# Layer 0's second and third modulation banks: 64 TensorE products per layer replaced by VectorE sums in the loaded tiles

## The chip, the core and the metric

The kernel runs on one core of a Trainium2 chip. A core has a matrix engine (TensorE, PE in the profile; its weight loads are the rows PEld), a vector engine (VectorE, DVE), a scalar engine (ScalarE, ACT), GpSimd (POOL) and a queue engine that issues most transfers (SyncE, SP). Each engine works through its own list of instructions in order and waits on semaphores. The metric is the device time of one execution in microseconds.

## The reference

Two decoder layers on 512 tokens of width 1024, in fp32. Each layer first makes six modulation rows of width 1024 from one conditioning vector `c`, and it is this product that the change touches:

```python
cond = jax.nn.silu(c)
mod = cond @ w_ada[l] + b_ada[l]              # w_ada[l]: 1024 x 6144
sh1, sc1, g1, sh2, sc2, g2 = jnp.split(mod, 6)
h = x * (1 + sc1) + sh1
y = hybrid_mixer(h, ...)                      # w_in, three token mixers, w_out
x = layer_norm(alpha * x + g1 * y)
h = x * (1 + sc2) + sh2
x = layer_norm(alpha * x + g2 * conv_ffn(h))
```

The mixer has a gated MLP, a retention (four chunks) and a sparse attention with eight heads, and ends in the product with w_out. In layer 0, `sh1` and `sc1` are needed at the very start, `sh2`, `sc2` (bank 1) and `g1`, `g2` (bank 2) only behind the mixer.

## The kernel before

Each weight tile of 128x1024 fp32 (512 KB) is loaded into one of three buffers `wraw` by SP (`Weights.load`, L102), and most are then split into a high part (ScalarE, L125) and a low part (VectorE or GpSimd, L127), so that three fast products give nearly fp32 accuracy. The modulation weights are used as they are loaded (jobs marked "raw"): row 8p+k of `w_ada` lies on partition p of tile k, so tile (k, h) holds one eighth of the contraction for the h-th 1024 columns of a bank.

`ada_bank` (L315) makes banks 1 and 2 of layer 0, 16 tiles each: for each tile, two fp32 products (L324) with `ce[:, k]` (silu of c) spread over 32 columns as the stationary side, 512 columns each, added up in PSUM over k. The four 512-wide pieces go to four 32-row strips of one PSUM bank. `ada_finish` (L357) adds the bias, and for bank 1 transposes.

These steps are fillers: `attention()` yields pieces of the attention (32 units: 4 head pairs, 2 branches, 4 row blocks; scores L944 to L946, row maximum L952, exponential L955, scaling L959, transposes L990, product with the values L998), between which `filler()` puts one piece of the retention (projections L535 to L537, chunks L881 to L920) and, at the places of `ADA_AT`, one modulation step. Attention looks two units ahead (`LOOK`). The unit whose row block is the first stands for both branches (L970 to L982). The written order is then rearranged by the framework's own scheduler, which puts instructions on each engine by its estimate of when they are ready; so the order on an engine is not that of the text.

`ada_dve` (L328) makes the banks of layer 1 another way, inside layer 0's feed-forward stage: GpSimd issues the loads, VectorE multiplies and adds each tile into an accumulator (L340, L342), and one product per strip with a column of ones sums over the partitions (L346).

The order of jobs for SP's queue: the eight tiles of the retention's projections (`rq` to `rg`) with the 32 modulation tiles between and behind them, then eight of w_out.

Of the kernel before, what the change touches and what calls it, by code (L numbers as in the profile page):

```python
# [14 lines left out]
OP = mybir.AluOpType  # L15
AX = mybir.AxisListType

P = 128
# [3 lines left out]
KD = D // P  # L22
# [126 lines left out]
def tile_trunk(ctx, tc, I, tab, out, layers=L):  # L149
    nc = tc.nc  # L150
    V, A, G, T = nc.vector, nc.scalar, nc.gpsimd, nc.tensor
# [6 lines left out]
    def ps():  # L158
        return psum.tile([P, 512], F32, tag="ps", name="ps")

    def t2(dt=F32):
        return pool.tile([P, 512], dt, tag="t2", name="t2", bufs=4)
# [44 lines left out]
    ADA_RUNS = {0: (0, D), 1: (3 * D, 4 * D), 2: (2 * D, 5 * D)}  # L207
# [9 lines left out]
    def ada_jobs(l, bank):  # L217
        wa = I["w_ada"][l].rearrange("(p k) n -> p k n", k=KD)
        return [(("ada", l, bank, k, h), "raw", [(lambda t: t[:, :D], wa[:, k, c0:c0 + D])])
                for k in range(KD) for h, c0 in enumerate(ADA_RUNS[bank])] + [None, None]  # L220

    def job_tm(key, l, parts):
        for h in range(2):
# [8 lines left out]
    for l in range(layers):  # L232
# [13 lines left out]
        for b, c0 in enumerate((C_KSL, C_KWN)):  # L246
            job_cols(("k", l, b), l, [(c0, P)])
        aj = [j for bank in (1, 2) for j in ada_jobs(l, bank)] if l == 0 else []
        for n in range(32):
            if n % 8 in (0, 2):  # L250
                nm, c0 = (("rq", C_QB), ("rk", C_KB), ("rv", C_VB), ("rg", C_GB))[n // 8]
                h = n % 8 // 2
# [14 lines left out]
    ws = Weights(nc, wpool, jobs)  # L267
# [5 lines left out]
    ce = const.tile([P, KD], F32, name="ce")  # L273
# [29 lines left out]
    ones = const.tile([P, 32], F32, name="ones")  # L303
# [10 lines left out]

    def ada_bank(l, bank):  # L315

        pm = ps()
        bt = ada_bias(l, bank)
        for k in range(KD):
            for h in range(2):  # L320
                raw = ws.next(("ada", l, bank, k, h))
                for a2 in range(2):
                    a = 2 * h + a2
                    T.matmul(pm[32 * a:32 * a + 32, :], ce[:, k:k + 1].to_broadcast([P, 32]), raw[:, a2 * 512:(a2 + 1) * 512],  # L324
                             start=(k == 0), stop=(k == KD - 1), tile_position=(0, 32 * a))
                yield
        yield from ada_finish(l, bank, pm, bt)

# [22 lines left out]
    def ada_bias(l, bank):  # L351
        bt = pool.tile([P, 512], F32, tag="adab", name="adab", bufs=1)
        for a in range(4):
            c0 = ADA_RUNS[bank][a // 2] + 512 * (a % 2)
            nc.gpsimd.dma_start(bt[32 * a:32 * a + 32, :], I["b_ada"][l][None, c0:c0 + 512].to_broadcast([32, 512]))
        return bt

    def ada_finish(l, bank, pm, bt):
        ms = pool.tile([P, 512], F32, tag="modg", name="modg", bufs=1) if bank == 2 else bt
        V.tensor_tensor(ms, pm, bt, op=OP.add)  # L360
        res = ms
        yield
        if bank != 2:

            pc = ps()
            for j in range(4):
                T.transpose(pc[:, j * P:(j + 1) * P], ms[:, j * P:(j + 1) * P], ident)
            res = pool.tile([P, 2, KD], F32, tag="modc", name="modc", bufs=3)
            V.tensor_copy(res.rearrange("p s (a j) -> p (s a) j", j=4),
                          pc.rearrange("p (j s x) -> p s j x", j=4, s=4)[:, :, :, 0])  # L370
            V.tensor_scalar(res[:, 1, :], res[:, 1, :], 1.0, None, op0=OP.add)
        ada_out[l, bank] = res
        yield
# [135 lines left out]
    for l in range(layers):  # L509
# [77 lines left out]
        else:  # L587
# [20 lines left out]
            def start_acc(k):  # L608

                r = raws.pop(k)  # L610
                acc = pt()[:, :256].rearrange("p (s n) -> p s n", s=2)
                for k2 in range(KD):
                    if k2 == 0:
                        V.tensor_scalar(acc, r[:, 0], ce[:, 0:1], None, op0=OP.mult)
                    else:
                        V.scalar_tensor_tensor(acc, r[:, k2], ce[:, k2:k2 + 1], acc, op0=OP.mult, op1=OP.add)
                return acc
# [36 lines left out]
            for k in range(KD):  # L654
# [7 lines left out]
                if k + 1 < KD:  # L662
                    ws.split(k + 1)
                    acc = start_acc(k + 1)
# [562 lines left out]
        for ct in range(NFF):  # L1227
# [8 lines left out]
            for b in range(2):  # L1236
                pa = pas[b]
                a = t2()
# [136 lines left out]
```

## Time and profile before

| | us |
|---|---|
| median of 3 runs (lowest, highest) | 1427.34 (1426.94, 1430.43) |
| the profiled execution, its own time | 1429.17 |
| its span, from the first to the last instruction | 1427.2 |
| PE busy in the span | 1368.5 |
| DVE busy | 889.6 |
| ACT busy | 549.4 |
| POOL busy | 213.8 |

A busy share is an average over stages with different limits; stages are told apart by the views of a stretch of time (counted in us from the span's start). The stage of the change runs from about 117 us, where the attention of layer 0 begins, to 324 us, where the residual add behind w_out begins.

### The profile page before, as it was taken

Reading aid. Unit: us, or ns where it says so; the run is one execution under the profiler, and the core shown is the slowest. Engines: PE = TensorE matmul, PEld = TensorE weight load, DVE = VectorE, ACT = ScalarE, POOL = GpSimd, SP = SyncE. Lnnn points to the kernel's source line nnn. Section 1 sums busy time; section 2 is a strip of 40 time slices with the busy share of each in tenths; the row PEclk is TensorE's granted clock in tenths of the full one; section 3 lists DMA queues with packets and bytes.
Section 4 is the critical chain, followed back from the end, with each engine's and each line's share of the span. In section 5 each row is a group of like instructions: output and inputs, shape, how many; then the busy total and the mean of one; then the engine's idle time right before and its main releaser. Section 6 shows DMA issues by size and latency. Waiting matters only on the chain.

```text
span 1427.2 us, 19802 instructions
## 1 busy us (share of the span) xinstructions
PE 1368.5 (96%) x7794; PEld 1126.6 (79%) x7794; DVE 889.6 (62%) x1463; ACT 549.4 (38%) x999; POOL 213.8 (15%) x212
## 2 busy tenths in 40 slices
PE   6999999999899999999999989999999999999995
PEld 5898665679887788778879978877898888888884
DVE  6658436757899566843466577486566555764337
ACT  2425333552443343333324245456243334343220
POOL 0311220335211010000030023111510000000005
PEclk9999999999999999999999999999999999999998
DMA  9822454513988354422514131110323334332221
GB/s 280 220 71 89 148 163 155 170 47 91 315 283 265 99 170 124 142 92 89 149 29 118 43 103 45 45 45 30 89 62 94 97 95 127 96 125 90 102 75 59
DMA packets 188012, 168.91 MB, mean 118 GB/s; under 512 B 23526, under 2 KB 167758, under 8 KB 187920
## 3 DMA queue, kind: packets, MB, share of 16 engines
q1 hardware_dynamic: 180368, 141.18, 33.0%
q0 software_dynamic: 7552, 26.48, 5.5%
q8 instruction: 61, 1.00, 0.3%
q14 instruction: 31, 0.25, 0.1%
HBM read 163.44 MB, written 2.10 MB: 116 GB/s over the span
## 4 chain that ended last, share of the span: by engine, by line
PE 83%; DVE 7%; DMA 4%; issue 2%; POOL 1%; ACT 1%; SPq 1%; DVEq 0%; ACTq 0%; POOLq 0%
PE ps L446 19%; PE ps L447 19%; PE ps L445 19%; PE ps L535 4%; PE ps L536 4%; PE ps L537 4%; PE ps L998 3%; PE ps L324 2%; PE ps L990 2%; DMA a<-in_w_ada_dram 1%; PE ps L944 1%; PE ps L506 1%; PE ps L945 1%; DMA wraw<-in_w_up_dram 1%; PE ps L431 1%
## 5 line engine op out<-in xcount | busy, mean ns | idle before, releaser
L125 ACT CAST whi<-wraw 128x1024 fp32r<-128x1024 f32 (+4 forms) x188 | 186.6, 997 | 390.7 <-PE ps L446 208.2
L127 DVE TENSOR_TENSOR wlo<-wraw,whi 128x1024 fp32r<-128x1024 f32 (+3 forms) x162 | 187.4, 1159 | 184.0 <-ACT whi L125 183.6
L447 PE MATMUL ps<-h2h,wlo 128*128 128x512 f32 (+1 forms) x736 | 278.8, 379 | 0.0
L446 PE MATMUL ps<-h2l,whi 128*128 128x512 f32 (+1 forms) x736 | 277.6, 377 | 0.0
L445 PE MATMUL ps<-h2h,whi 128*128 128x512 f32 (+1 forms) x736 | 277.5, 378 | 0.0
L445 PEld LDWEIGHTS ps<-h2h,whi 128*128 128x128 f32 x736 | 138.9, 189 | 28.4 <-ACT whi L125 2.5
L446 PEld LDWEIGHTS ps<-h2l,whi 128*128 128x128 f32 x736 | 139.0, 189 | 27.1
L447 PEld LDWEIGHTS ps<-h2h,wlo 128*128 128x128 f32 x736 | 139.0, 189 | 26.1 <-issue 0.8
L535 PE MATMUL ps<-whi,hh 128*128 128x256 f32 (+1 forms) x448 | 131.7, 294 | 0.0
L536 PE MATMUL ps<-wlo,hh 128*128 128x256 f32 (+1 forms) x448 | 128.1, 286 | 0.0
L537 PE MATMUL ps<-whi,hl 128*128 128x256 f32 (+1 forms) x448 | 127.5, 285 | 0.0
L1141 POOL TENSOR_TENSOR xa<-xa,t 128x256 f32<-128x256 f32 (+1 forms) x30 | 35.8, 1200 | 527.2 <-DVE t L1140 527.2
L446 PE MATMUL ps<-wlo,pt 128*128 128x512 f32 x288 | 113.9, 396 | 0.0
L445 PE MATMUL ps<-whi,pt 128*128 128x512 f32 x288 | 113.9, 396 | 0.0
L447 PE MATMUL ps<-whi,pt 128*128 128x512 f32 x288 | 111.8, 396 | 0.0
L535 PEld LDWEIGHTS ps<-whi,hh 128*128 128x128 f32 x448 | 85.6, 191 | 15.2 <-issue 11.7
L536 PEld LDWEIGHTS ps<-wlo,hh 128*128 128x128 f32 x448 | 85.5, 191 | 3.6 <-issue 3.5
L537 PEld LDWEIGHTS ps<-whi,hl 128*128 128x128 f32 x448 | 85.4, 191 | 0.2 <-issue 0.2
L127 POOL TENSOR_TENSOR wlo<-wraw,whi 128x1024 fp32r<-128x1024 f32 x26 | 62.5, 2406 | 142.7 <-ACT whi L125 142.7
L187 DVE TENSOR_TENSOR pt<-g,pt 128x512 fp32r<-128x512 f32 x32 | 22.1, 691 | 81.5 <-PE ps L446 79.9
L991 ACT COPY pT<-ps 128x128 f32<-128x128 f32 (+3 forms) x128 | 50.2, 438 | 53.3 <-PE ps L990 52.9
L955 ACT ACTIVATE pt<-ps,sm 128x256 f32<-128x256 f32 (+2 forms) x96 | 55.8, 590 | 37.3 <-DVE sm L952 26.1
(272 smaller groups left out, 2682.4 us busy)
## 6 DMA issues: line engine op xcount, KB each, us to landing
wraw<-in_w_up_dram SPq DMA_DIRECT2D x88, 512.0 KB, 3.9
araw<-in_w_ada_dram POOLq DMA_DIRECT2D x48, 512.0 KB, 5.9
wraw<-in_w_down_dram SPq DMA_DIRECT2D x44, 512.0 KB, 3.5
wraw<-in_w_ada_dram SPq DMA_DIRECT2D x32, 512.0 KB, 3.4
wraw<-in_w_in_dram SPq DMA_DIRECT2D x30, 512.0 KB, 3.6
wraw<-in_w_out_dram SPq DMA_DIRECT2D x16, 512.0 KB, 4.1
a<-in_w_ada_dram SPq DMA_DIRECT2D x14, 512.0 KB, 7.2
wraw<-in_w_in_dram SPq DMA_DIRECT2D x8, 384.0 KB
```

The lines of the kernel that those rows point to most:

```text
L125: self.nc.scalar.copy(f(hi), src)
L127: eng.tensor_tensor(f(lo), src, f(hi).bitcast(F32), op=OP.subtract)
L445: T.matmul(o, lh, rh, start=first, stop=False)
L446: T.matmul(o, lh, rl, start=False, stop=False)
L447: T.matmul(o, ll, rh, start=False, stop=last)
L535: T.matmul(o, a, wh[:, k - k0, :], start=(first and k == 0), stop=False)
L536: T.matmul(o, a, wl[:, k - k0, :], start=False, stop=False)
L537: T.matmul(o, b, wh[:, k - k0, :], start=False, stop=(last and k == KD - 1))
L955: A.activation(pp[e][:, :n], o[e], AF.Exp, bias=sm[:, 0, e:e + 1], accum_out=sm[:, 1, e:e + 1])
L991: A.copy(PT[e][:, i:i + 3 * i + 1:3, :], pb[:, :(i + 1) * P].rearrange("p (j q) -> p j q", q=P))
L998: T.matmul(po[64 * e:64 * e + 64, j * P:], VS[:, b, j, 64 * g:64 * g + 64], PT[e][:, 4 * j:4 * j + NT - j, :].rearrange("p a q -> p (a q)" ...
L1141: eng.tensor_tensor(X[t][:, c0:c0 + n], X[t][:, c0:c0 + n], tmp, op=OP.add)
```

## The change

The steps of a bank are put in another order (all eight k of the first half of the columns, then all eight of the second, instead of both halves for each k), and so are their loads. VectorE multiplies the first tile of a half by `ce[:, 0]` in place (L325 of the changed kernel), and for each later tile writes `tile * ce[:, k] + sum so far` into the later tile (L327), so that the sum moves on from buffer to buffer. Behind the eighth tile, two products with a 128x32 block of ones (L333) sum over the partitions. `loads=2` lets one tile be loaded ahead of a step where it was two. Lines behind the change have numbers higher by 9.

```diff
-                for k in range(KD) for h, c0 in enumerate(ADA_RUNS[bank])] + [None, None]
+                for h, c0 in enumerate(ADA_RUNS[bank]) for k in range(KD)] + [None, None]
...
-        pm = ps()
+
         bt = ada_bias(l, bank)
-        for k in range(KD):
-            for h in range(2):
-                raw = ws.next(("ada", l, bank, k, h))
-                for a2 in range(2):
-                    a = 2 * h + a2
-                    T.matmul(pm[32 * a:32 * a + 32, :], ce[:, k:k + 1].to_broadcast([P, 32]), raw[:, a2 * 512:(a2 + 1) * 512],
-                             start=(k == 0), stop=(k == KD - 1), tile_position=(0, 32 * a))
+        pm = None
+        for h in range(2):
+            acc = None
+            for k in range(KD):
+                raw = ws.next(("ada", l, bank, k, h), loads=2)
+                if acc is None:
+                    V.tensor_scalar(raw, raw, ce[:, 0:1], None, op0=OP.mult)
+                else:
+                    V.scalar_tensor_tensor(raw, raw, ce[:, k:k + 1], acc, op0=OP.mult, op1=OP.add)
+                acc = raw
+                if k == KD - 1:
+                    pm = pm or ps()
+                    for a2 in range(2):
+                        a = 2 * h + a2
+                        T.matmul(pm[32 * a:32 * a + 32, :], ones, acc[:, a2 * 512:(a2 + 1) * 512],
+                                 start=True, stop=True, tile_position=(0, 32 * a))
                 yield
```

What that makes of the order shows at three places. First PE, in the second half of the stage, behind the value products of a head pair (L1005, in the changed kernel L1014): before, the modulation products L324 stand between the retention's (L892, L901, L907) and the transposes (L990) and scores (L944) of the attention.

```order
L1005 MATMUL ps<-pcT,vcs 64x512 x2
L892 MATMUL ps<-t_2342 128x128 x4
L901 MATMUL ps<-vb,rot 64x64 x4
L324 MATMUL ps<-wraw,ce 32x512 x2
L990 MATMUL ps<-tb,pt 128x128 x2
L324 MATMUL ps<-wraw,ce 32x512 x4
L907 MATMUL ps<-vb,t_2371 128x64
L944 MATMUL ps<-kh,q_601 128x512
L945 MATMUL ps<-kl,q_601 128x512
```

The same place in the changed kernel:

```order
L1014 MATMUL ps<-pcT,vcs 64x512 x2
L901 MATMUL ps<-t_2320 128x128 x4
L910 MATMUL ps<-vb,rot 64x64 x4
L999 MATMUL ps<-tb,pt 128x128 x2
L916 MATMUL ps<-vb,t_2351 128x64
L953 MATMUL ps<-kh,q_601 128x512
L954 MATMUL ps<-kl,q_601 128x512
```

The three modulation steps are gone, and the rest stands closer together. Second VectorE, from the mask of the gated MLP (L792) and the low parts of the keys (L187) to the row maxima of the first attention units (L975, L949, L952) and the first scaling (L982). Before:

```order
L792 TENSOR_TENSOR t_1170<-ps,tb 128x512
L187 TENSOR_TENSOR kl<-ps,kh 64x512 x4
L801 SCALAR_TENSOR_TENSOR U<-ps,pcol,U 128x4x64
L187 TENSOR_TENSOR kl<-ps,kh 64x512 x2
L801 SCALAR_TENSOR_TENSOR U<-ps,pcol,U 128x4x64 x3
L187 TENSOR_TENSOR kl<-ps,kh 64x512 x2
L975 TENSOR_REDUCE sm<-ps 128x4
L949 TENSOR_REDUCE sm<-ps 128x2
L952 TENSOR_REDUCE sm<-ps 128x1 x2
L979 RECIPROCAL sm<-sm 128x4
L982 TENSOR_SCALAR pt<-pt,sm,gates 128x128 x4
```

In the changed kernel, from the same mask (now L801) on:

```order
L801 TENSOR_TENSOR t_1170<-ps,tb 128x512
L327 SCALAR_TENSOR_TENSOR wraw<-wraw,ce 128x1024
L187 TENSOR_TENSOR kl<-ps,kh 64x512 x2
L327 SCALAR_TENSOR_TENSOR wraw<-wraw,ce 128x1024
L810 SCALAR_TENSOR_TENSOR U<-ps,pcol,U 128x4x64 x3
L187 TENSOR_TENSOR kl<-ps,kh 64x512 x2
L810 SCALAR_TENSOR_TENSOR U<-ps,pcol,U 128x4x64
L327 SCALAR_TENSOR_TENSOR wraw<-wraw,ce 128x1024
L187 TENSOR_TENSOR kl<-ps,kh 64x512 x2
L984 TENSOR_REDUCE sm<-ps 128x4
L958 TENSOR_REDUCE sm<-ps 128x2
L961 TENSOR_REDUCE sm<-ps 128x1 x2
```

Three steps (k = 2, 3, 4 of the first half of bank 1) have moved in here; k = 0 and k = 1 stand ahead of it, and k = 5 right behind its last row, still ahead of the first scaling. Third VectorE where bank 1 ends and bank 2 begins (L360 adds the bias of bank 1). Before:

```order
L952 TENSOR_REDUCE sm<-ps 128x1 x2
L956 RECIPROCAL sm<-sm 128x2
L959 TENSOR_SCALAR pt<-pt,sm,gates 128x512 x2
L360 TENSOR_TENSOR adab<-ps,adab 128x512
L949 TENSOR_REDUCE sm<-ps 128x2
L956 RECIPROCAL sm<-sm 128x2
L959 TENSOR_SCALAR pt<-pt,sm,gates 128x256 x2
```

In the changed kernel:

```order
L327 SCALAR_TENSOR_TENSOR wraw<-wraw,ce 128x1024
L961 TENSOR_REDUCE sm<-ps 128x1
L327 SCALAR_TENSOR_TENSOR wraw<-wraw,ce 128x1024
L961 TENSOR_REDUCE sm<-ps 128x1
L325 TENSOR_SCALAR wraw<-wraw,ce 128x1024
L965 RECIPROCAL sm<-sm 128x2
L968 TENSOR_SCALAR pt<-pt,sm,gates 128x512 x2
L369 TENSOR_TENSOR adab<-ps,adab 128x512
L958 TENSOR_REDUCE sm<-ps 128x2
L327 SCALAR_TENSOR_TENSOR wraw<-wraw,ce 128x1024
L965 RECIPROCAL sm<-sm 128x2
L968 TENSOR_SCALAR pt<-pt,sm,gates 128x256 x2
```

Four steps now stand between the row maxima and the scalings of two attention units. SP's queue issues the same modulation tiles at the same places among the tiles of w_in.

## Rows read from the trace of the kernel before

**Rows 1.** The page: busy time, and the chain that ended last by engine.

```profile
PE 1368.5 (96%) x7794; PEld 1126.6 (79%) x7794; DVE 889.6 (62%) x1463; ACT 549.4 (38%) x999; POOL 213.8 (15%) x212
PE 83%; DVE 7%; DMA 4%; issue 2%; POOL 1%; ACT 1%; SPq 1%; DVEq 0%; ACTq 0%; POOLq 0%
```

**Rows 2.** Stretches of the stage: length, busy time by engine, clock, DMA share, GB/s.

```profile
117.00:145.00 28.00, 27.80 (x175) 23.32 (x172) 23.10 (x58) 16.20 (x44) 6.17 (x4) 1.00 0.21 66
145.00:167.00 22.00, 22.00 (x131) 13.32 (x129) 10.05 (x29) 8.02 (x20) 5.99 (x4) 1.00 0.49 156
167.00:202.00 35.00, 35.00 (x228) 23.43 (x228) 16.22 (x46) 11.04 (x32) 7.12 (x6) 1.00 0.51 161
202.00:231.00 29.00, 29.00 (x192) 20.19 (x191) 12.86 (x25) 9.48 (x24) 6.86 (x6) 1.00 0.48 152
231.00:258.00 27.00, 26.07 (x180) 13.72 (x178) 15.21 (x37) 11.67 (x35) 0.00 (x0) 1.00 0.61 197
258.00:278.00 20.00, 19.93 (x158) 15.23 (x156) 15.83 (x40) 12.78 (x36) 11.39 (x9) 1.00 0.65 195
...
sum 207.00, PE 202.56 PEld 142.12 DVE 119.08 ACT 93.35 POOL 48.73; mean PE 25.32 PEld 17.77 DVE 14.88 ACT 11.67 POOL 6.09
```

**Rows 3.** The same stretches, L324 alone: length, PE, PEld.

```profile
202.00:231.00 29.00, 6.19 (x24) 0.74 (x22) 1.00 0.48 152
231.00:258.00 27.00, 10.09 (x44) 1.44 (x44) 1.00 0.61 197
258.00:278.00 20.00, 1.49 (x7) 0.14 (x4) 1.00 0.65 195
sum 207.00, PE 33.64 PEld 4.58; mean PE 4.21 PEld 0.57
```

**Rows 4.** Timeline of PE at one modulation step: start, length, instruction, idle before.

```profile
144.03 1.05 PE L324 MATMUL ps<-wraw,ce 128*32 128x512 f32 x4
145.01 0.19 PEld L536 LDWEIGHTS ps<-wlo,hh 128*128 128x128 f32 x1 [0.84 <-issue]
```

**Rows 5.** Lines L342 and L340, layer 1's modulation on VectorE: ns min/median/max.

```profile
L342 DVE SCALAR_TENSOR_TENSOR acc<-araw,ce,acc x42: 1265/1274/1287, 359.0 to 577.0; 128x1024 f32<-128x1024 f32 x42
L340 DVE TENSOR_SCALAR acc<-araw,ce x6: 741/744/802, 357.4 to 508.5; 128x1024 f32<-128x1024 f32 x6
```

**Rows 6.** Loads: median us to landing (page and DMA view), then SP's timeline.

```profile
wraw<-in_w_ada_dram SPq DMA_DIRECT2D x32, 512.0 KB, 3.4
...
wraw<-in_w_in_dram SPq DMA_DIRECT2D x9, 512.0 KB, 4.4
...
116.05 0.33 SPq L102 DMA_DIRECT2D wraw<-in_w_ada_dram  x1
...
120.60 5.82 SPq L102 DMA_DIRECT2D wraw<-in_w_ada_dram  x2
```

**Rows 7.** Timeline: VectorE's first scaling, and PE's first transposes behind it.

```profile
137.34 1.11 DVE L982 TENSOR_SCALAR pt<-pt,sm,gates 128x128 f32<-128x128 f32 x4
...
139.58 0.38 PE L990 MATMUL ps<-tb,pt 128*128 128x128 f32 x2
```

**Rows 8.** PE's timeline at a later stall, and the stretches behind it.

```profile
366.54 1.97 PE L431 MATMUL ps<-tb,xa 128*128 128x128 f32 x8 [3.98 <-DVE xa L1151]
...
365.00:370.00 5.00, 3.46 (x16) 3.46 (x17) 3.96 (x5) 0.46 (x1) 1.14 (x2) 0.50 1.04 322
370.00:375.00 5.00, 5.00 (x37) 5.00 (x36) 4.12 (x7) 2.52 (x5) 1.06 (x2) 0.81 0.98 336
```

**Rows 9.** Timeline: a split on GpSimd beside VectorE; both lines' groups (count, busy, mean).

```profile
317.33 2.42 POOL L127 TENSOR_TENSOR wx<-wraw,wx 128x1024 fp32r<-128x1024 f32 x1 [1.99 <-ACT wx L125]
...
318.65 1.64 DVE L187 TENSOR_TENSOR yl<-yc,yh 128x512 fp32r<-128x512 f32 x1 [9.46 <-ACT yh L1088]
...
L187 DVE TENSOR_TENSOR yl<-yc,yh 128x512 fp32r<-128x512 f32 x3 | 2.0, 681 | 0.4 <-ACT yh L1088 0.4
...
L127 POOL TENSOR_TENSOR wlo<-wraw,whi 128x1024 fp32r<-128x1024 f32 x8 | 19.1, 2382 | 40.1 <-ACT whi L125 40.1
```

## The prediction

> **What bounds the kernel now.** I read the page first: PE is busy for 96% of the span and makes up 83% of the chain that ended last [rows 1], so time can only be won where PE gets less to do or waits less. Then I cut the stage of the change, 117 to 324 us, at the places where an attention branch's last unit is scaled, and asked for every engine's busy time in each stretch. PE is busy for 202.56 of 207 us, VectorE for 119.08, so VectorE has 88 us to spare over the stage; but not evenly: 23.10 of 28 us in the first stretch, 10.05 of 22 in the second, 15.83 of 20 in the stretch from 258 us [rows 2]. The same cut for the modulation products alone gives 33.64 us of PE, 10.09 of them between 231 and 258 us [rows 3]. In PE's timeline a step's products start at 144.03 and the next weight load stands at 145.01 with nothing that it waits for but PE's own issue [rows 4]: a step occupies PE for about 1.05 us (33.64/32) and nothing runs beside it there. So the removed work lies on the path, in a stage where PE is the bound at full clock (1.00 in every row). Last I looked for what would be late next: the loads, which have three buffers, and VectorE's place in the order ahead of the first scaling.
>
> **The change part by part.** *Removed on PE.* Of 32 steps of two products, 4 stay as products with ones, of the same shape on both sides, so the same 1.05 us each. 28 x 1.05 = 29.4 us come off PE. This is also the most that the change can give.
>
> *Added on VectorE.* 28 multiply-adds and 4 multiplications of 128x1024 fp32. The nearest rows are the same operations at the same size, 1274 and 744 ns [rows 5]: 28 x 1.274 + 4 x 0.744 = 38.6 us. Over the stage VectorE goes from 119 to 158 us, and PE from 202.6 to 173. It fits in sum, so I don't take VectorE as the bound of the whole stage. Two stretches are another matter, since an instruction that waits for its tile holds up everything behind it on VectorE.
>
> *The start.* Counting in the changed order, six steps (k = 0 to 5) stand ahead of the first scaling, where none did. Their tiles don't come in time. The second is issued at 120.60 [rows 6] and lands some 3.4 us later, so its step ends at about 125.3. A buffer now comes free only when the next step has read the sum in it, and the third buffer is taken by a tile of w_in in its split: so from there each load is issued when the step before has ended, and each step costs load and sum in a row, 3.4 + 1.27 + about 0.1 = 4.8 us. Step k = 5 ends at 125.3 + 4 x 4.8 = 144.5. Behind it stand two reciprocals and six rotations of the retention, some 1.5 us. The first scaling moves from 137.34 [rows 7] to about 146. PE's first transposes, at 139.58 [rows 7], have the same place in PE's order and wait for it: 8.8 us lost. Bounds: nothing, if SP got the tiles so early that the steps fit into VectorE's gaps (28 - 23.10 = 4.9 us of them, [rows 2]), and 15 us if every load took the 4.4 us of a w_in tile [rows 6] and k = 6 were waited for too. I take 8.8, since the load's own row is the nearer one.
>
> *The clock.* [...] I add one such fall behind the start's wait: 3.4 us; bounds 0 and 10 (three falls).
>
> *The change of banks.* From 202 to 278 us PE is busy for 29.00 + 26.07 + 19.93 = 75.0 us [rows 2], less 6.19 + 10.09 + 1.49 = 17.8 of modulation [rows 3], plus three product steps of 1.05: 60.4. VectorE is busy for 43.9 there, and 20 of the 32 steps fall into it by the changed order (7, 8 and 5, two of them multiplications): 18 x 1.274 + 2 x 0.744 = 24.4, so 68.3 us. VectorE is longer by 8 us. Against that stands that it is shorter than PE by some 14 us in the two stretches before (26.3 and two steps of 2.0, against 57 less 14.9), of which the two units of look-ahead keep perhaps half. I take 5 us, between 0 and 12 (8 and one wait for tile, split and tile behind the w_in tiles that are loaded there).
>
> *Queues.* ScalarE's splits of w_in tiles wait for loads that now follow VectorE's steps, and its exponentials are queued behind them; GpSimd's subtractions meet the steps. Together I take 3 us, between -2 (loads of w_in come earlier in places, since PE no longer frees them) and 8.
>
> [...] A subtraction of two SBUF tiles on VectorE, beside a split on GpSimd that ran from 317.33 to 319.75, took 1.64 us, where three such took 681 ns on average [rows 9]. [...] The added multiply-adds have two SBUF inputs. [...]
>
> *Sum.* 29.4 - 8.8 - 3.4 - 5 - 3 = 9.2 us. Against the profiled execution's own time of 1429.17 (span 1427.2) that is 1420.0; it lies 1.8 us above the median of the runs, so for the median 1427.34 - 9.2 = **1418**. Its own range, from the terms' nearer bounds, is 1409 to 1427. Bank 2's late end costs nothing: its rows are wanted at 324 us. Behind the stage I expect no change: the order there is nearly the same.
>
> **Rivals.** *All of PE's gain is kept* (VectorE and the loads are hidden by the look-ahead): 1427.3 - 29.4 = 1398, with a first wait of a few us 1402. For it: 88 us of slack on VectorE [rows 2]. Against it: six steps ahead of the first scaling, and 4.8 us for each.
>
> *The waits eat it*: each of eight splits holds VectorE by its 2.38 us [rows 9], where one of them cost the row beside it 0.96. Then VectorE is 19 us longer in the two crowded parts and nothing of the 29.4 is left with the start (8.8) and its clock (3.4): 1427.3 - 29.4 + 31.3 = 1429, with some of the splits outside the crowded parts 1427. For it: VectorE is at 83% of the first stretch before anything is added. [...]
>
> *The loads set the pace, and it gets slower.* If tiles come one at a time all along, 31 steps of 4.8 us follow the first landing at 119.5, and the six w_in tiles between them add load and split, 4.4 + 2.42 = 6.8 each: 119.5 + 148.8 + 40.8 = 309 us for the last step, which has its place at about 278. Then 31 us are lost: 1458; with half of the w_in tiles hidden, 289, and 1438. It decides from 278 on: (278 - 119.5 - 20)/31 = 4.5 us for a step and its load. Against it: behind the start two loads are often under way, since two buffers come free in turn.
>
> **How the numbers follow.** Forecast 0.56, all gain kept 0.14, waits eat it 0.16, loads set the pace 0.14. A difference of 0.3%, 4.3 us, is what a measurement of this kernel can tell from no change: so faster means below 1423, slower above 1431.6. Faster: 0.14 and 0.48 of the forecast's 0.56, that is 0.62. Same: 0.08 of the forecast and 0.14 of the third case, 0.22. Slower: 0.14 and 0.02, 0.16. The range from 1404 to 1434 leaves out most of the first rival (0.1) and nearly all of the last (0.12).
>
> **What would show it.** L324 gone from PE, four steps of about 1.05 us in its place; VectorE's multiply-adds at 1.27 us, some stretched to 2 or 3 beside GpSimd's splits. The first transposes of the stage at about 148 us instead of 139.58, with VectorE waiting for `wraw` tiles ahead of it, steps 4.8 us apart from k = 1 to k = 5, and a clock of 0.50 right behind. PE about 60 us busy between the bias of bank 1 and the last step, with VectorE at 90% or more. The add behind w_out at about 315 us instead of 324. If the first transposes come before 142 us, the loads were quicker than I say and the time goes towards 1400; if VectorE waits for tiles to the end of bank 2, towards 1440.

## The result: 0.7% slower, and the profile after

The changed kernel takes 1440.72 us (median of 5, 1434.64 to 1441.86), the kernel before 1430.37 on the same chip; the ratio is 1.0071 with a 95% interval of 1.0055 to 1.0086. The forecast was 1418, with a range of 1404 to 1434, so it was wrong in size and in sign. The profiled execution of the changed kernel is the quickest of its five, 1434.64 us at a mean granted clock of 0.977 where the other four had 0.970 to 0.972. Against the profiled execution before (1429.17) it is 5.5 us longer, where the medians differ by 10.4; what the other four lost beyond it is in no trace. All lines behind the change are now 9 higher (L982 is L991, L1166 is L1175).

Of these 5.5 us, 3.65 were lost ahead of the change. On PE, VectorE, ScalarE and GpSimd both traces have the same instructions in the same order up to the first sum, yet GpSimd's first split of the stage starts that much later. Before, then changed:

```profile
118.16 2.41 POOL L127 TENSOR_TENSOR wlo<-wraw,whi 128x1024 fp32r<-128x1024 f32 x1 [7.49 <-ACT whi L125]
```

```profile
121.81 2.41 POOL L127 TENSOR_TENSOR wlo<-wraw,whi 128x1024 fp32r<-128x1024 f32 x1 [7.49 <-ACT whi L125]
```

The granted clock was 0.94 up to 60 us and 0.91 from 80 to 100 us in the changed kernel's execution, and 1.00 in the other. Of the versions below, `order_loads`, `no_products` and `nl_before` also have the kernel before's order up to this split and start it at 119.81, 119.98 and 121.66, so such a spread comes without the change. Some comparisons below are therefore counted from this split.

The page of the changed kernel, busy time and the chain by engine, answers to [rows 1]:

```profile
PE 1350.5 (94%) x7682; PEld 1129.7 (79%) x7682; DVE 928.9 (65%) x1495; ACT 548.4 (38%) x999; POOL 220.5 (15%) x212
PE 79%; DVE 9%; DMA 5%; issue 2%; ACT 1%; POOL 1%; SPq 1%; DVEq 0%; POOLq 0%; ACTq 0%
```

PE has 18 us less to do and VectorE 39 more, but VectorE and the DMAs have moved into the chain (7 to 9%, 4 to 5%). Next the groups of the new lines within 117 to 324 us (count, busy time, mean ns, idle before and its cause):

```profile
L327 DVE SCALAR_TENSOR_TENSOR wraw<-wraw,ce 128x1024 f32<-128x1024 f32 x28 | 39.7, 1417 | 13.5 <-DMA wraw<-in_w_ada_dram 11.7 <-issue 1.5
L325 DVE TENSOR_SCALAR wraw<-wraw,ce 128x1024 f32<-128x1024 f32 x4 | 5.5, 1364 | 3.2 <-DMA wraw<-in_w_ada_dram 3.2
L333 PE MATMUL ps<-wraw,ones 128*32 128x512 f32 x16 | 4.7, 676 | 0.0
```

The removed work is as worked out: 33.64 us [rows 3] less 4.7 is 28.9 (all of it in layer 0: 64 products, for which 8 with ones are left). The added work is 45.2 us instead of 38.6, and in front of it VectorE stood idle for 14.9 us until tiles landed. The same stretches as in [rows 2] (length, busy time by engine, clock, DMA share, GB/s):

```profile
117.00:145.00 28.00, 22.91 (x117) 19.24 (x116) 22.01 (x34) 13.63 (x27) 7.32 (x3) 0.88 0.43 131
145.00:167.00 22.00, 18.61 (x133) 16.40 (x131) 19.83 (x44) 10.45 (x34) 4.90 (x3) 0.92 0.49 143
167.00:202.00 35.00, 35.00 (x249) 27.73 (x248) 28.28 (x70) 12.97 (x39) 11.72 (x8) 1.00 0.46 136
202.00:231.00 29.00, 27.17 (x204) 22.87 (x203) 18.03 (x27) 12.53 (x34) 6.86 (x6) 1.00 0.52 158
231.00:258.00 27.00, 17.19 (x120) 11.68 (x120) 26.30 (x45) 10.57 (x32) 0.00 (x0) 0.81 0.45 134
258.00:278.00 20.00, 18.73 (x145) 14.03 (x145) 18.72 (x41) 11.60 (x27) 8.78 (x7) 1.00 0.60 182
sum 161.00, PE 139.61 PEld 111.95 DVE 133.17 ACT 71.75 POOL 39.59; mean PE 23.27 PEld 18.66 DVE 22.19 ACT 11.96 POOL 6.60
```

The two stretches behind, of the changed kernel and then of the kernel before:

```profile
278.00:292.00 14.00, 8.83 (x52) 5.79 (x52) 12.12 (x27) 7.49 (x24) 4.76 (x4) 0.88 0.33 101
292.00:324.00 32.00, 29.25 (x204) 22.25 (x202) 13.48 (x30) 16.59 (x42) 7.11 (x3) 1.00 0.14 43
```

```profile
278.00:292.00 14.00, 12.17 (x83) 8.45 (x83) 13.69 (x33) 9.83 (x30) 1.65 (x1) 1.00 0.01 2
292.00:324.00 32.00, 30.59 (x219) 24.45 (x218) 12.12 (x22) 14.33 (x32) 9.57 (x4) 1.00 0.21 67
```

These rows settle the account of this trace. Before, PE was idle for 1.2 of the 161 us, and for 1.8 and 1.4 us in the two stretches behind, always at a clock of 1.00: 4.4 us. Now it is idle for 21.4, 5.2 and 2.7: 29.3 us. The clock column adds time at a clock of 0.50: in windows of 1 us it reads 0.50 from 131 to 136, 154 to 157, 236 to 246 and 284 to 287 us and 1.00 otherwise, but for the window at each change. That is (1 - 0.88) x 2 x 28 = 6.7 us in the first row, 3.5 in the second, 10.3 in the fifth and 3.4 in the row from 278, together 23.9 us. One product (L455) took 628 ns on average at 0.50 (132.5 to 136.2 us) and 391 at 1.00 (137.2 to 140 us); if all of PE's work took twice as long at 0.50, half of the 23.9 us, 12, would be lost, an estimate for the most that the clock cost. So 24.9 us of idle time and up to 12 us of clock stand against 28.9 won. Two VectorE lines of the changed kernel's timeline, the fourth scaling and the add behind w_out:

```profile
281.60 1.11 DVE L991 TENSOR_SCALAR pt<-pt,sm,gates 128x128 f32<-128x128 f32 x4
...
330.79 0.69 DVE L1175 TENSOR_TENSOR t<-ps,grow 128x512 f32<-128x512 f32 x1 [3.39 <-PE ps L456]
```

and the same two of the kernel before:

```profile
280.68 1.10 DVE L982 TENSOR_SCALAR pt<-pt,sm,gates 128x128 f32<-128x128 f32 x4
...
323.68 0.69 DVE L1166 TENSOR_TENSOR t<-ps,grow 128x512 f32<-128x512 f32 x1 [3.39 <-PE ps L447]
```

Counted from the split, the fourth scaling comes 2.7 us earlier than before (159.8 for 162.5), so up to there the sums had won a little, and the add comes 3.5 us later (209.0 for 205.5). From the one to the other it took 43.0 us before and 49.2 after: 6.2 us lost in a stretch that holds no sum at all. Behind the add 1.6 us come back, since the adds are 7.1 us apart and the spans 5.5. The stage thus lost 3.5 us net, so 32.4 in all; 24.9 of them are idle time, which by estimate leaves 7.5 for the clock.

How the start was lost is read in the timeline of the changed kernel from 127 us, GpSimd, VectorE and PE (start, length, instruction, idle before):

```profile
127.31 2.55 POOL L127 TENSOR_TENSOR wlo<-wraw,whi 128x1024 fp32r<-128x1024 f32 x1 [3.09 <-ACT whi L125]
...
127.86 3.09 DVE L327 SCALAR_TENSOR_TENSOR wraw<-wraw,ce 128x1024 f32<-128x1024 f32 x1 [0.20 <-issue]
130.87 0.41 DVE L724 TENSOR_TENSOR pt<-pt,tb 128x256 f32<-128x256 f32 x1
...
134.71 1.28 DVE L327 SCALAR_TENSOR_TENSOR wraw<-wraw,ce 128x1024 f32<-128x1024 f32 x1 [0.62 <-DMA wraw<-in_w_ada_dram]
...
139.67 1.28 DVE L327 SCALAR_TENSOR_TENSOR wraw<-wraw,ce 128x1024 f32<-128x1024 f32 x1 [2.24 <-DMA wraw<-in_w_ada_dram]
...
150.01 1.28 DVE L327 SCALAR_TENSOR_TENSOR wraw<-wraw,ce 128x1024 f32<-128x1024 f32 x1
...
152.52 1.10 DVE L991 TENSOR_SCALAR pt<-pt,sm,gates 128x128 f32<-128x128 f32 x4
...
131.42 1.09 PE L733 MATMUL ps<-tb,pt 128*128 128x128 f32 x4 [5.09 <-DVE pt L724]
...
152.91 0.33 PE L999 MATMUL ps<-tb,pt 128*128 128x128 f32 x1 [1.83 <-DVE pt L991]
```

From the third on the sums come about 5 us apart, as forecast. But VectorE waits only 0.62 and 2.24 us for landings here, and PE's longest wait has another cause: the second sum, beside a split of GpSimd, takes 3.09 us and holds a small product (L724) behind it, for which PE waits 5.09 us. The first transposes come at 152.91 instead of 139.58 [rows 7], 9.7 us later when counted from the split.

Where the banks change, the loads and the sums take turns. In the chain that ended last, from 202 to 278 us, landings of modulation tiles have 25.6% and the sums 15.7% (before: landings 6.5%, the products 19.5%). Pieces of this chain (start, length, what):

```profile
214.82 5.86 DMA wraw<-in_w_ada_dram
220.71 1.29 DVE wraw L327
222.02 3.60 DMA wraw<-in_w_ada_dram
225.64 1.28 DVE wraw L327
226.95 4.15 DMA wraw<-in_w_ada_dram
```

Each load here is issued when a sum ends, and a later sum waits for its landing.

### The profile page after: what moved, and what is told of

It reads as the page before. It is cut to its first block, busy times and chain, and to the rows that moved or that the text cites. A ratio compares the mean times of both kernels' runs of the same rounds, so it can differ in the third digit from the quotient of the medians.

```text
span 1432.7 us, 19615 instructions
## 1 busy us (share of the span) xinstructions
PE 1350.5 (94%) x7682; PEld 1129.7 (79%) x7682; DVE 928.9 (65%) x1495; ACT 548.4 (38%) x999; POOL 220.5 (15%) x212
## 4 chain that ended last, share of the span: by engine, by line
PE 79%; DVE 9%; DMA 5%; issue 2%; ACT 1%; POOL 1%; SPq 1%; DVEq 0%; POOLq 0%; ACTq 0%
PE ps L454 20%; PE ps L456 19%; PE ps L455 19%; PE ps L544 3%; PE ps L545 3%; PE ps L546 3%; PE ps L1007 3%; DMA wraw<-in_w_ada_dram 2%; PE ps L999 1%; DVE wraw L327 1%; PE ps L515 1%; DVE pt L968 1%; PE ps L953 1%; DMA wraw<-in_w_in_dram 1%; SPq L184 1%
## 5 line engine op out<-in xcount | busy, mean ns | idle before, releaser
L455 PE MATMUL ps<-h2l,whi 128*128 128x512 f32 (+1 forms) x736 | 277.6, 378 | 0.0
L455 PEld LDWEIGHTS ps<-h2l,whi 128*128 128x128 f32 x736 | 139.0, 189 | 27.2
L456 PEld LDWEIGHTS ps<-h2h,wlo 128*128 128x128 f32 x736 | 139.0, 189 | 26.1 <-issue 0.8
L455 PE MATMUL ps<-wlo,pt 128*128 128x512 f32 x288 | 113.9, 395 | 0.0
L187 DVE TENSOR_TENSOR pt<-g,pt 128x512 fp32r<-128x512 f32 x32 | 22.1, 690 | 81.6 <-PE ps L455 80.0
L1249 ACT ACTIVATE t<-ps,pcol 128x512 f32<-128x512 f32 x88 | 68.1, 774 | 1.7 <-PE ps L456 1.7
```

Of the source, the lines that this page charges most:

```text
L455: T.matmul(o, lh, rl, start=False, stop=False)
L456: T.matmul(o, ll, rh, start=False, stop=last)
L1249: A.activation(a, pa, AF.Identity, bias=cwc[:, 3, cx:cx + 1], scale=cwc[:, 2, cx:cx + 1])
```

## Experiments

Ratios are to the kernel before on the same chip, with their 95% intervals; differences between versions in us are differences of these ratios. Every edit shifts the scheduler's whole order of instructions, and `ADA_AT` also places the modulation tiles among SP's loads, so no edit below changes one thing alone. Two things in that order matter below: how many sums stand ahead of the first scaling (none before, 6 in the changed kernel), and where in PE's queue the last scores of layer 0's fourth head pair stand, in rows ahead of that pair's end (97 before, 53 in the changed kernel).

**First round: a fourth tile, and later sums.** `c_before`, `c_after` and `e_four` have one 'p' and one 't2' buffer fewer; `e_four` spends the room on a fourth `wraw` buffer and loads two ahead.

```
-PB = 5                                  +PB = 4
-tag="t2", name="t2", bufs=4             +tag="t2", name="t2", bufs=3
-tag="wraw", name="wraw", bufs=3         +... bufs=4      (e_four)
-ws.next(("ada", l, bank, k, h), loads=2) +ws.next(("ada", l, bank, k, h), loads=3)   (e_four)
```

> A control: the kernel before with one buffer fewer of the 'p' tiles (5 to 4) and of the 't2' tiles (4 to 3), which frees 4 KB of a partition. No theory of the change says anything of it. If the two tiles have slack it comes out within 0.3% of the kernel before (1426 to 1434 us); what it costs beyond that is taken off the next two kernels.

> The changed kernel with the same two buffers fewer. Every theory: slower than the control of before by the same 0.7% (0.4 to 1.0%), first scaling L991 at 150 to 155 us.

> The changed kernel with those two buffers fewer, the 4 KB given to a fourth arriving tile (wraw) and two loads ahead of a step as before. Theory 1 (loads one at a time: a step's load waits for the step before it, VectorE waits at the head of its queue for the landing): steps at the start come every 2 to 3 us instead of 4.8, the idle time of VectorE for in_w_ada landings falls from 15 us to under 6, the first scaling comes 8 to 12 us earlier than in the changed kernel, and the time falls by 8 to 14 us below the changed kernel with the same buffers, to 0.5% or so under the control of before. Theory 2 (the 38.6 us of VectorE's own work in a crowded stage): the work is the same, so the time stays within 0.3% of the changed kernel with the same buffers.

Measured: 1.0072 [1.0052, 1.0091], 1.0089 [1.0074, 1.0104] and 1.0080 [1.0065, 1.0095]. The control failed: the two buffers alone cost 10 us (with them gone the last scores stand 49 rows ahead). The traces have 3.2 us (`c_before`) and 8.8 us (`c_after`) more behind the add than the kernel before, so not all of it lies in the stage. `c_after` is 0.17% above its control, where every theory had 0.4 to 1.0%. `e_four` is 0.09% under `c_after`, within the noise, but ten sums then stood ahead of the first scaling, at 155.3. So this says nothing on the loads; the control drew attention to the end of PE's queue.

```
-    ADA_AT = [n for n in range(4, 60) if n % 8 != 7]
+    ADA_AT = [n for n in range(10, 70) if n % 8 != 7]     (e_late10; 12 in late12)
```

> The changed kernel with the first sum placed six retention steps later (the list ADA_AT starts at 10 instead of 4), so that 2 instead of 6 sums stand ahead of the first scaling on VectorE; buffers and loads as changed. Theory 1 with the loss at the start: first transposes about 8 us earlier (145 instead of 153), time 5 to 10 us under the changed kernel, unless the sums that now stand later, one load at a time, take it back between 270 and 325 us. Theory 2: the same work on VectorE, only later, where it is as crowded: within 0.3% of the changed kernel. A third theory, the order in which PE's products now stand (nothing to do with VectorE): no change either.

Measured: 1427.61 us, 0.9966 [0.9953, 0.9979], first scaling at 142.0. The same sums, six steps later, are 15 us less than in the changed kernel and faster than before; in the traces the add comes 4.9 us earlier than in the changed kernel. The gain is more than the 5 to 10 us forecast for the start, and the row count of the last scores had also changed, to 91. VectorE's waits for landings grew meanwhile. The view of waits, 120 to 290 us (total, times, longest), of the changed kernel and then of this one:

```profile
DVE wraw L327 <- DMA wraw<-in_w_ada_dram: 11.7, 10, 5.1
```

```profile
DVE wraw L327 <- DMA wraw<-in_w_ada_dram: 17.0, 11, 3.5
```

So VectorE's total of waits does not decide. That what stands behind the waiting instruction does is the likely reading, not a shown one.

**Second round: the end of PE's queue.** `tail_after` is the changed kernel with `range(5, 70)`, `tail_before` the kernel before with `range(6, 70)`, `order_loads` the kernel before with the loads half by half and `loads=2`.

> The changed kernel with every ada step one retention step later (ADA_AT starts at 5 instead of 4): still six sums ahead of the first scaling on VectorE and one load at a time, but in PE's queue the last scores of layer 0's fourth head pair stand where the kernel before has them, 97 rows ahead of the end of that pair instead of 53. Theory A (a first part of the loss at the start, where the steps' loads wait for the sums; a second part, some 6 us, from the order in which PE's queue ends the attention): first scaling still at 150 to 155 us, residual add 5 to 7 us earlier than in the changed kernel, time 1432 to 1436 us, ratio to before 1.001 to 1.004. Theory B (loads one at a time and VectorE's work alone; the order at the end costs nothing): as the changed kernel, ratio 1.006 to 1.008.

> The kernel before, products on PE as before, with every ada step two retention steps later (ADA_AT starts at 6): no sum on VectorE, but PE's queue ends the attention in the changed kernel's order (last scores 50 rows ahead of the end of the fourth pair instead of 97). Theory A: residual add 4 to 7 us later than before, time 1434 to 1438 us, ratio 1.003 to 1.006. Theory B: nothing in it that VectorE or the loads have to wait for, so within 0.2% of before (1427 to 1433 us).

> The kernel before with the products left on PE, but the banks' tiles loaded half by half and one load ahead instead of two, as in the changed kernel; the order of the end of the attention stays that of before. Theory A and B: the loads get into a row only because the next one waits for the sum in a buffer; where PE reads each tile and frees it at once they don't, so 1427 to 1434 us, first scaling at 137 to 139. A third theory (the fewer loads ahead by themselves delay the input tiles behind them in SP's queue): 5 us or more slower than before, first transposes late.

> The changed kernel with the steps eight retention steps later (ADA_AT starts at 12): two sums ahead of the first scaling, and the end of the attention in the order of before (98 rows). Theory A: neither of the two losses, as in the one that starts at 10: 1422 to 1430 us, ratio 0.994 to 0.999. Theory B without a loss at the start would give the same. If sums crowd VectorE between 230 and 285 us instead (fall of the granted clock there, fourth scaling at 284 or later), 1428 to 1434 us.

Measured: 1.0026 [1.0010, 1.0041], 1.0025 [1.0009, 1.0041], 1.0020 [1.0006, 1.0035], 0.9995 [0.9981, 1.0009]. The first two cross over as theory A says, by 6.4 and 3.6 us where theory B had 0, the second ratio just below A's range. But the mark that theory A named in the traces was missed in both: the add was to come 5 to 7 us earlier than in the changed kernel and 4 to 7 us later than before. It came at 328.20 and 325.14, 2.6 us earlier and 1.5 us later. Counted from the split it came 1.0 us later than in the changed kernel, and 1.2 us later than before. PE's timeline shows how the end differs. First the changed kernel:

```profile
308.73 2.37 PE L1007 MATMUL ps<-pT,vs 128*64 128x512 f32 x14
...
311.65 0.48 PE L953 MATMUL ps<-kh,q 128*128 128x512 f32 x1
...
316.00 1.08 PE L999 MATMUL ps<-tb,pt 128*128 128x128 f32 x8 [2.33 <-DVE pt L968]
...
323.37 1.07 PE L1014 MATMUL ps<-pcT,vcs 64*64 64x512 f32 x4
```

then `tail_after`:

```profile
301.14 2.37 PE L1007 MATMUL ps<-pT,vs 128*64 128x512 f32 x14
...
305.42 0.47 PE L953 MATMUL ps<-kh,q 128*128 128x512 f32 x1
...
313.39 1.08 PE L999 MATMUL ps<-tb,pt 128*128 128x128 f32 x8 [0.79 <-DVE pt L968]
...
320.77 1.08 PE L1014 MATMUL ps<-pcT,vcs 64*64 64x512 f32 x4
```

From the last scores (L953) to the last transposes (L999) the softmax has 8.0 us in `tail_after`, which PE fills with products of w_out. In the changed kernel it has 4.4, PE waits for it, and those products are left over for the time behind the pair. So from the fourth scaling to the add `tail_after` takes 43.0 us, as the kernel before. But its fourth scaling is at 285.19, counted from the split 7.2 us later than in the changed kernel: in these two traces the loss has changed its place. That the order at the end by itself is worth 6 us is not shown. Part of the 6.4 us between the medians goes with the granted clock of the executions: at 0.972 two of `tail_after` took 1438.3 and 1439.1 us, and one of the changed kernel 1440.7. `order_loads` costs 2.9 us at a first scaling of 139.0: with the tiles read by PE, loading one ahead is cheap. `late12` came 0.7 us above its first expected range, with the fourth scaling at 279.9, so not for the reason given there: one place of the steps is not like another, and I have not followed it up.

**Third round: what can be had.** `no_products` leaves 28 of 32 product pairs out; the two `nl_` kernels leave the 32 loads out and read a tile of x, so in all three the modulation is not computed; `half10` has its steps from 10 on and sums only h = 0 on VectorE.

```
-                for a2 in range(2):
+                for a2 in range(2 if k == 0 else 0):             (no_products)
-                raw = ws.next(("ada", l, bank, k, h), loads=2)
+                raw = X[0]                                       (nl_after; nl_before alike)
```

> The kernel before with its loads of the two banks, but 28 of the 32 pairs of products left out (only k = 0 is kept), and nothing put on VectorE: what the freed PE time is worth with no sum in its place. If PE's time is the path all through the stage: 29.4 us less, about 1401 us (1398 to 1405), ratio 0.979. If the softmax on VectorE and ACT or the tiles' arrival sets the pace as soon as PE has less to do: 1408 to 1418 us, and the difference to 1401 was never to be had.

> The kernel before without the 32 loads of the two banks: the products stay on PE and read a resident tile of x instead, so the modulation is not computed. Every theory: the loads are hidden there, 1425 to 1432 us; it is the base for the next run.

> The changed kernel without the 32 loads of the two banks: the sums are done in place in a resident tile of x, so the modulation is not computed; the sums cost VectorE the same 38.6 us, but none waits for a landing. Seven of them stand ahead of the first scaling. Theory A1 (a sum's price is its load: VectorE stands at the head of its queue until the tile lands): first scaling at 141 to 147 instead of 152, and 12 us or more faster than the run without loads that keeps the products (ratio 0.990 or less). Theory A2 (a sum's price is its own 1.27 us in a crowded VectorE): first scaling at 146 to 152, and within 5 us of the run without loads that keeps the products.

> The changed kernel with steps from 10 on and only the first half (h = 0) of each bank summed by VectorE, the second half left to PE's products: 14 steps removed from PE (14.7 us), some 19 us added to VectorE; two sums ahead of the first scaling, the end of the attention in the order of before (99 rows). Theory A (what late sums lose is the crowded VectorE between 230 and 285 us, where each step is worth less than it costs): as fast as the one with all sums from 10 on, or faster: 1422 to 1428 us. Theory B (PE's time is worth its full length wherever it goes): 10 us slower than that one, 1432 to 1438 us.

Measured: 0.9824 [0.9802, 0.9846], 0.9928 [0.9905, 0.9952], 0.9854 [0.9826, 0.9881], 1.0020 [1.0003, 1.0036]. The removed PE time is worth 25 of its 29 us, between the two cases expected. The loads are not free before either: 10 us, where I expected none. Without loads, the sums still win only 0.9854/0.9928, 0.75% or 10.6 us; by the difference some 14 of the 25 us would go for the sums' own time on VectorE, if the two pairs may be compared although `no_products` keeps the loads. `nl_after` met neither theory whole: its first scaling is at 143.0 as A1 has it, its gain lies between the two. It also is no clean test of the start, as its VectorE timeline shows: with nothing to land, the first eight sums went to a place long before the stage (here the first of them).

```profile
66.14 0.75 DVE L325 TENSOR_SCALAR xa<-xa,ce 128x1024 f32<-128x1024 f32 x1
```

`half10` is 7.7 us above `e_late10`, nearer to theory B (10) than to A (0 or less): the 14.7 us of products that it leaves on PE are worth, net of the sums that they replace, about half their length there; that VectorE's crowd makes late sums worthless has fallen.

**Fourth round: first sums, GpSimd, and the late version again.** `first_resident` has its steps from 5 on, like `tail_after`, and takes the eight tiles of (bank 1, h = 0) from x, without their loads, so that half is not computed. `no_lock` moves layer 0's eight splits of the retention's tiles from GpSimd to VectorE (first edit), `late10_bias` has its steps from 10 on and the bias rows on SyncE's queue (second edit):

```
-eng = self.nc.gpsimd if key[0] in self.on_pool else self.nc.vector
+eng = self.nc.gpsimd if key[0] in self.on_pool and key[:2] not in (("rq", 0), ("rk", 0), ("rv", 0), ("rg", 0)) else self.nc.vector
-            nc.gpsimd.dma_start(bt[32 * a:32 * a + 32, :], ...)
+            nc.sync.dma_start(bt[32 * a:32 * a + 32, :], ...)
```

> The changed kernel, steps from 5 on as in tail_after, but the eight sums of the first half of the first bank are done on a resident tile of x, without their loads (that half of the modulation is not computed); the other 24 sums load as changed. Theory A1 (what the first sums cost the start is the wait for their loads at the head of VectorE's queue): first scaling at 142 to 147 instead of 154, and 6 to 10 us faster than tail_after, ratio to before 0.995 to 0.999. Theory A2 (it is their own time on VectorE, eight times 1.27 us): first scaling at 150 or later and 1.001 to 1.004, as tail_after.

> The changed kernel with the eight splits of layer 0's retention inputs (rq, rk, rv, rg) on VectorE instead of GpSimd, so that no split runs beside the sums until w_out's; the first sums and the end of PE's queue stand as in the changed kernel. Theory C (a split on GpSimd holds VectorE, and this is a good part of the loss): faster than the changed kernel by 3 us or more, ratio to before 1.005 or less. Theory A: the stretch saved (6 us of VectorE in the trace) is about what eight more splits cost VectorE, and neither is where the loss is: 1.006 to 1.012.

> The version of the changed kernel that starts its steps at 10, run again beside the next one: 0.995 to 0.998 of before if its gain stands; 0.999 to 1.001 if it was this chip's draw.

> late10 with the modulation's four bias rows a bank loaded through SyncE's queue instead of GpSimd's, so that the fourth scaling, which stood 6.2 us beside the bias DMAs and two splits of GpSimd, has less of GpSimd beside it. Theory C (GpSimd's run of work held VectorE there): the longest scaling under 4 us, 2 to 5 us faster than late10, ratio 0.993 to 0.996. Theory A, where the place of the sums decides: as late10, 0.996 to 0.998.

Measured: 0.9905 [0.9888, 0.9922], 1.0016 [1.0006, 1.0027], 0.9976 [0.9966, 0.9987], 0.9962 [0.9949, 0.9975]. The first eight sums with their loads, out of the stage, are worth 17 us over `tail_after`, and PE waits 0.4 us between 117 and 170 where it waited 8.4 in the changed kernel. Here too the scheduler put them at 65 to 95 us, so wait and work of these sums are not told apart; only their place is shown to cost.

`no_lock` is 7.9 us faster than the changed kernel, with eight more splits on VectorE and the same end of PE's queue, as theory C has it. In the traces, counted from GpSimd's last step ahead of the splits (L480, at 111.09 and 112.67), its add comes only 1.4 us earlier; so the traces show what a split does to a sum, not that this is 7.9 us. One case stands in the changed kernel's timeline, GpSimd's split and VectorE's multiplication, which takes 0.745 us alone:

```profile
204.86 2.38 POOL L127 TENSOR_TENSOR wlo<-wraw,whi 128x1024 fp32r<-128x1024 f32 x1 [10.56 <-ACT whi L125]
...
205.00 2.79 DVE L325 TENSOR_SCALAR wraw<-wraw,ce 128x1024 f32<-128x1024 f32 x1 [3.16 <-DMA wraw<-in_w_ada_dram]
```

It begins in the split and ends 0.55 us behind it. In `no_lock` no sum is longer than 1286 ns, and the stretches from 202 to 258 us, where three sums in a row had lost time (two to splits, one to a load behind them), read:

```profile
202.00:231.00 29.00, 29.00 (x219) 24.45 (x217) 20.31 (x35) 12.41 (x32) 2.08 (x4) 1.00 0.62 189
231.00:258.00 27.00, 22.22 (x161) 16.09 (x160) 26.93 (x50) 12.58 (x38) 0.00 (x0) 0.94 0.46 135
```

against 27.17 and 17.19 of PE at 1.00 and 0.81. But the first scaling came later still, at 157.7, and from 117 to 167 us PE is busy for 35.9 us where the changed kernel has 41.5, so much of the gain is lost there. `late10b` confirms the late version's gain; `late10_bias` is the fastest that computes all, 0.38% under before. Its longest scaling (a piece of L991) took 2.46 us, where `late10b` had 6.26, as theory C has it, but the intervals of the two overlap, so the step from one to the other is not settled.

**Last: all three mended.** `three_quarters` has both edits of the fourth round, steps from 7 and the first half of bank 1 on PE; `late10_both` is `late10_bias` with the splits of `no_lock`.

```
+                summed = (bank, h) != (1, 0)
+                raw = ws.next(("ada", l, bank, k, h), loads=2 if summed else 3)
+                if not summed:
+                    ...                        # before's products
```

> A version meant to beat both: the first half of the first bank is left to PE's products (steps from 7 on), the other 24 sums are VectorE's, layer 0's retention splits are VectorE's instead of GpSimd's, the bias rows come through SyncE's queue; the end of the attention in before's order (97 rows), no sum ahead of the first scaling. If the three losses (first sums' loads, end order, splits on GpSimd) are the whole of it: 21 us of products removed, less some 10 us for the sums' own time on VectorE later: 1418 to 1424 us, ratio 0.990 to 0.995. If the gain of the late version came from something else: as late10_bias or slower, 0.996 or more.

> late10_bias with layer 0's retention splits on VectorE instead of GpSimd as in no_lock; three sums ahead of the first scaling, last scores 71 rows ahead of the end of the fourth pair. If GpSimd's splits hold VectorE in the late version as in the changed one: 3 to 6 us faster than late10_bias, 0.991 to 0.995. If the splits stood beside no sum there (the longest sum in late10_bias took 1.39 us), the eight splits only add to VectorE: 0.997 to 1.002.

Measured: 1.0114 [1.0099, 1.0128] and 0.9981 [0.9972, 0.9991]. Neither gives the gain that it was built for. `late10_both` falls into its second case: it is 2.7 us above `late10_bias`, with intervals that overlap, and in `late10_bias` no sum met a split (1389 ns at most), so that moving splits only adds to VectorE. `three_quarters` is the slowest version of all. Its profile has PE at 20.27, 20.44 and 14.50 us busy of 27, 25 and 22 from 231 to 305 us at clocks of 0.77 to 0.81. PE waits there for several VectorE lines, most for one of the retention (L911, 11.0 us in four waits), and I have not found one cause. So the gains of the three edits don't add up.

## Why the prediction was wrong

The forecast took 20.2 us of losses off the 29.4; the trace has 32.4 us of losses against 28.9 won. By the terms of the sum:

*Removed on PE*: right, 28.9 us measured for 29.4; its worth without any sum is 25 (22 to 28 by the interval).

*Start*: the size right, the mechanism in part. From the third sum on the steps came 4.8 to 5.5 us apart, and the first transposes came 9.7 us later where 8.8 was forecast. By the windows PE had 8.3 us more idle time than before and lost up to 5.1 us by the clock (the estimate above) up to 167 us, 13.4 for the forecast 8.8 + 3.4. But VectorE waited for landings for only 2.9 us ahead of the first scaling, and PE's longest wait (L733, 5.09) came from the second sum, stretched beside a split; so the agreement is partly luck. Moved late, the sums gave 0.5 to 0.6% over `tail_after`, 7 to 9 us.

*Clock*: one fall of 3.4 taken, bound 10. No run shows what a fall costs; the 3.4 are my estimate from the clocks in [rows 8], with time lost in proportion to the clock. The trace of the changed kernel has four falls in the stage, 6.7, 3.5, 10.3 and 3.4 us at a clock of 0.50, 23.9 in all, of which the account above leaves 7.5 as lost, by estimate; the term was less than half of it.

*Change of banks*: the first step that failed. I compared busy times, 68.3 us of VectorE to 60.4 of PE, and took 5 us. VectorE was busy for 63.1 there, since 16 sums fell into it and not 20 (by the forecast's own count six, not two, were left for the two stretches before; ten came there behind the first scaling). Yet PE was idle for 12.9 us (1.0 before), and the clock took up to 5 more by the same estimate. A sum of busy times doesn't see loads and sums that take turns, nor single waits in an order: VectorE stood 3.16 us for a tile and then under a split, the next sum took 3.35 us beside another split, and the third waited 5.07 for its tile.

*Queues, 3 us*: probably too small. Three sums beside a split took 3.09, 2.79 and 3.35 us, where the same took 1.28, 0.745 and 1.28 alone: 5.9 us on VectorE (a fourth lost 0.4), at four of eight splits. In `no_lock`, without these splits on GpSimd, no sum took over 1.29 us, and the version won 7.9 us by the medians and 1.4 in the traces. The rival had 2.38 us for each of eight splits, 19 in all; the loss was real, but met few.

*End of the attention*: the second step that failed, a term put at nothing without a reason. The prediction looked at the order behind the stage, where 1.6 us came back, and not at PE's order from 278 us to the add. The last scores stood 53 rows ahead of the pair's end there and not 97, PE was idle for 7.9 us where it had been for 3.2, and the way from the fourth scaling to the add took 6.2 us more. `tail_after` undid these 6.2 us in its trace but lost 7.2 ahead of them, so whether the order at the end is the cause stays open.

Of the rivals, "loads set the pace" had the side right, and its mechanism for a part: loads and sums took turns ahead of the first scaling and again from 207 to 242 us, but not all along, and the last sum began at 264.8, ahead of its place at 278. "Waits eat it" was right that nothing is left of the gain, but it was by waits of three kinds and not by splits alone.

Open stays what the changed kernel's four untraced executions lost beyond the traced one, 6 to 7 us; how much of the first sums' price is the wait and how much their own time, since each kernel without the wait had the sums elsewhere; and what `three_quarters` lost.

## What to carry to other kernels

Before two traces are compared, find an instruction ahead of the change that both have, and count times from it: here 3.65 of 5.5 us were lost before the change began. Work moved from a full engine to a half-empty one is paid for at the places where it stands in that engine's queue: list what the bottleneck engine waits for behind each moved instruction, and the waits for its tile, before summing busy times. When a scheduler sets the order, compare the whole order up to the next barrier, not only the lines of the edit; here an edit of one number, the first step's place, was worth 14 to 15 us, more than the change. And give a chained sum its own timing against the loads: in the crowded stretches each load was issued only when a sum had ended.

## What the runs showed of the hardware

A VectorE instruction lasted through more than one of GpSimd's. In `e_late10` the fourth scaling, 0.34 us a piece by the median, stood beside four DMA issues and two splits of GpSimd in a row. GpSimd, then VectorE:

```profile
276.85 2.04 POOL L364 DMA_DIRECT2D adab<-in_b_ada_dram  x4
278.90 4.65 POOL L127 TENSOR_TENSOR wlo<-wraw,whi 128x1024 fp32r<-128x1024 f32 x2
```

```profile
277.38 7.03 DVE L991 TENSOR_SCALAR pt<-pt,sm,gates 128x128 f32<-128x128 f32 x4
```

One of the four pieces took 6.26 us, from 277.38 till 0.1 us behind the end of the second split (283.55). It has one tile and per-partition factors as input. With the bias loads on SyncE's queue (`late10_bias`) no piece of this line took more than 2.46 us.
